# A two-layer decoder trunk: the gate and up products of the feed-forward by Strassen's scheme, with weight sums formed by accumulating DMAs

## The chip, the cores and the metric

The kernel runs on one core of one Trainium2 chip. The metric is the device time of one execution in microseconds, the median of several runs. The engines are TensorE (PE; PEld is its loading of weights), VectorE (DVE), ScalarE (ACT), GpSimd (POOL) and SyncE (SP, which here only issues transfers). All data are float32; products are made of operands split into a high and a low part of the type fp32r, with three matmuls (high x high, high x low, low x high) for each product.

## The reference

Two layers work on x, 512 tokens of 1024 features: each is a mixer, a norm, a feed-forward product and another norm. The change is in the feed-forward:

```python
def swiglu(x, w_gate, w_up, w_down):
    return (jax.nn.silu(x @ w_gate) * (x @ w_up)) @ w_down
...
for layer in range(DEPTH):                      # DEPTH = 2
    ...                                         # mixer: y from x
    x = layer_norm(ALPHA * x + y, ln_mix_g[layer], ln_mix_b[layer])
    x = layer_norm(ALPHA * x + swiglu(x, ffn_w_gate[layer], ffn_w_up[layer], ffn_w_down[layer]),
                   ln_ffn_g[layer], ln_ffn_b[layer])
```

w_gate and w_up are 1024 x 2816, w_down is 2816 x 1024. The 2816 hidden features are 22 tiles of 128 (KF = 22); the 1024 input features are 8 tiles (KD = 8).

## The kernel before, in words

x is kept transposed, features on partitions, as a high part `xh` and a low part `xl`, each 128 x 8 x 512, and in natural layout as `xn`. Weights come as pieces of 128 x 1024 (512 KB) in the order of their use. `fetch` loads the next one on SP's queue into one of five `raw` buffers; `split` has ACT cast it to the high part and DVE subtract that from the raw piece for the low part (lines 94 and 100; on POOL for the first three pieces after a norm, line 98); a pair of high and low lies in one of five `w` buffers.

In `ffn`, a hidden tile needs a gate piece and an up piece. `gemm_a` (line 176) makes the 24 matmuls of a piece, 8 input tiles by three parts, into one PSUM bank of 128 features x 512 tokens. The first two hidden tiles are done in halves of 256 tokens, because the last two blocks of tokens come late from the mixer's norm: the steps `flips` that transpose those blocks stand between their matmuls. The other 20 tiles take 48 matmuls of 512 columns each. `finish` makes the SwiGLU of the two banks (ACT's tanh, line 319, two operations on DVE, lines 320 and 321) and writes the hidden tile: the first eight to the large tile `m8`, the others to `wk` slots of 128 x 512. Then `down` (line 281) takes the hidden tiles as weights, in natural layout, and ends with the residual and `layer_norm`, whose `flip` transposes a finished block on TensorE, casts it from the bank on ACT (line 267) and subtracts on DVE (line 268).

TensorE works in the order in which the program is written. The order of the instructions on the other engines is laid down by a planner at compile time, from costs that it assumes; on the chip each engine then works in that fixed order and stops at an instruction whose operands are not there. Transfers are issued in order on the queue of the engine that starts them. There are eight PSUM banks.

Of the kernel before, what the change touches and what calls it, by code (L numbers as in the profile page):

```python
# [10 lines left out]
F32 = mybir.dt.float32  # L11
# [3 lines left out]
ALU = mybir.AluOpType  # L15
# [14 lines left out]
LOW = -3e38  # L30
VSTAT = (2, 3)  # the blocks whose norm takes its statistics on VectorE, not ScalarE
POOL = 3  # weights split on GpSimd after a norm
WARM = 8  # products of zeros that raise TensorE's clock while the first operands load
RAW, WP, WK, HX = 5, 5, 14, 11
LEVELS = (64, 32, 16, 8, 4, 2, 1)
# [8 lines left out]
def trunk(ctx, tc, a, out):  # L44
# [13 lines left out]
    tmp = ctx.enter_context(tc.tile_pool(name="tmp", bufs=4))  # L58
    sm = ctx.enter_context(tc.tile_pool(name="sm", bufs=4))
    psp = ctx.enter_context(tc.tile_pool(name="psp", bufs=8, space=bass.MemoryType.PSUM))  # L60

    cnt = [0]

    def nm(s):
        cnt[0] += 1
        return f"{s}{cnt[0]}"
# [9 lines left out]

    def small(shape, tag):
        return sm.tile(shape, F32, tag=tag, name=nm(tag))

    def ps():  # L80
        return psp.tile([P, 512], F32, tag="ps", name=nm("ps"))

# [1 line left out]
    state = {"i": 0, "pool": 0}  # L84
# [28 lines left out]
    def weave(*lists):  # L113
        """one order for several lists of steps, each spread evenly"""
        steps = [((i + 0.5) / len(l), n, f) for n, l in enumerate(lists) for i, f in enumerate(l)]
        for _, _, f in sorted(steps, key=lambda x: x[:2]):
            f()

# [1 line left out]
    xh = big.tile([P, KD, S], F32R, name="xh")  # L120
# [3 lines left out]
    def begin(banks):  # L124
        """the first two products, fed piece by piece as x and their weights arrive"""
        raws = [rawp.tile([P, D], F32, tag="raw", name=nm("raw")) for _ in range(2)]
        state["i"] = 2
        ws = [pair(), pair()]

        def load_w(f, half):  # L130
            c = slice(half * 512, half * 512 + 512)
            src = raws[f][:, c]
            nc.sync.dma_start(out=src, in_=a["w"][0, :, f * D + half * 512:f * D + half * 512 + 512])
            split(src, ws[f][0][:, c], ws[f][1][:, c])

# [12 lines left out]
        load_x(1)  # L148
        gemm_a(banks[0], ws[0], ks=(1,))
        load_w(1, 0)  # L150
        gemm_a(banks[1], ws[1], ks=(0, 1))
        for k in (2, 3):
            load_x(k)
            for f in range(2):
                gemm_a(banks[f], ws[f], ks=(k,))
        load_w(0, 1)
        load_w(1, 1)
        for k in range(4, KD):
            load_x(k)
            for f in range(2):  # L160
                gemm_a(banks[f], ws[f], ks=(k,))
        w = weight()
        nc.sync.dma_start(out=pack, in_=a["pack"])
        nc.sync.dma_start(out=wgate, in_=a["wgate"])
        nc.sync.dma_start(out=lm, in_=a["lmask"])
        nc.gpsimd.tensor_copy(out=lmask, in_=lm)
        tsc(out=nsink, in0=sinks, scalar1=-1.0, scalar2=None, op0=ALU.mult)
        return w

# [1 line left out]
    def gemm_a(dst, w, cols=slice(0, S), ks=range(KD)):  # L171
        """dst[128 features, tokens] += w^T x"""
        hi, lo = (t.rearrange("p (k m) -> p k m", k=KD) for t in w)
# [5 lines left out]
    def pieces_a(then, w=None):  # L179
        """two steps of a product whose bank goes to then()"""  # L180
        got = {}
# [10 lines left out]
    def pieces_b(n, then, first=1):  # L192
        """natural layout: a step for each block of tokens (or the first few together),
        x w with 128 tokens and n features"""
        ws = []
# [27 lines left out]

    def layer_norm(b, acc, gb, last):
        """the norm of a block; returns the step that transposes it"""
        g, be = gb
# [32 lines left out]
        def flip():  # L259
            for h in range(2):  # L260
# [6 lines left out]
                nc.scalar.copy(out=xh[dst], in_=tv)  # L267
                tt(out=xl[dst], in0=tv, in1=xh[dst].bitcast(F32), op=ALU.subtract)  # L268
        return flip

    def down(hs, groups, gb, last=False, after=None):
        """natural layout product over the tiles hs, the residual and the norm;
        returns the steps that transpose the last two blocks"""
        nk = len(hs)
# [16 lines left out]
        for gi, size in enumerate(groups):  # L291
            parts = [prep(k) for k in range(k0, k0 + size)]
            k0 += size
            for b in range(NB):
# [11 lines left out]
                if k0 == nk:  # L306
                    flips.append(layer_norm(b, acc[b], gb, last))
        state["pool"] = POOL
        return flips

    def ffn(layer, last, flips):
        gb = load_ln("ffn", layer)
        m8 = big.tile([P, 8, S], F32, tag="m8", name=nm("m8"))
        hs = []

        def finish(f, pg, pu):
            h = m8[:, f, :] if f < 8 else slot()
            t = temp()
# [7 lines left out]
        for f in range(2):  # L326
            for part in range(2):
# [4 lines left out]
                gemm_a(bank, w, cols=slice(0, 256), ks=range(4, KD))  # L332
                first.append((w, bank))
        for f in range(2):
            for w, bank in first[2 * f:2 * f + 2]:
                gemm_a(bank, w, cols=slice(256, 512))
            finish(f, first[2 * f][1], first[2 * f + 1][1])
        with tc.issue_after(norm.ins):
            w = weight()
        for f in range(2, KF):  # L340
            pg, pu = ps(), ps()
            gemm_a(pg, w or weight())
            w = None
            gemm_a(pu, weight())
            finish(f, pg, pu)
        return down(hs, [1] * (KF - 5) + [5], gb, last)

# [1 line left out]
    def mixer0():  # L349
# [113 lines left out]
        weave(att[1:], fill[4:])  # L463
        return down([mix[:, i, :] for i in (4, 5, 6, 7, 0, 1, 2, 3)], [4, 4], gb)

# [1 line left out]
    def rms_scale(ss, n, w):  # L467
# [6 lines left out]
    def mixer1(flips):  # L474
        mix = big.tile([P, 8, S], F32, tag="m8", name=nm("m8"))
        # latent projections, natural layout: [c_q 256 | c_kv 128 | k_r 32 | g_low 16]
        cq = [(slot2(F32R), slot2(F32R)) for _ in range(2)]
# [4 lines left out]
        def latent(b, bank):  # L482
# [10 lines left out]
            kr = mi[:, 384:416]  # L493
            t1, t2 = small([P, 32], "kr1"), small([P, 32], "kr2")
            nc.gpsimd.tensor_tensor(out=t1, in0=kr, in1=kcos[:, b, :], op=ALU.mult)
# [39 lines left out]

        # decay: log-sigmoid, summed within each block of 128
        bb = [slot2(), slot2()]
# [16 lines left out]

        # up-projections; the norms' gains scale the weights' rows
        def scaled(n, parts):
# [47 lines left out]

        # latent attention: a unit is a block of queries and two heads
        def latent_unit(i, hp):
# [76 lines left out]

        # gated linear attention: within blocks of 128, halves against halves at every scale,
        # each with exponents taken from the last token of the first half
        at = [slot2() for _ in range(4)]
        for h in range(4):  # sums of logarithms are never above 0: zeros
            nc.vector.tensor_scalar(out=at[h], in0=bb[h // 2], scalar1=0.0, scalar2=None, op0=ALU.is_gt)
# [47 lines left out]

        dq = small([P, 16], "dq")
        qb, kd = [slot(), slot()], [slot(), slot()]
        dec = [small([P, 4], "dec0"), small([P, 4], "dec1")]

# [94 lines left out]
        for c in range(3):  # L835
# [11 lines left out]
        return down([mix[:, i, :] for i in (4, 5, 6, 7, 0, 1, 2, 3)], [4, 4], gb,  # L847
                    after=[lambda: output_flip(2), lambda: output_flip(3)])

# [14 lines left out]
    sel, bgate, gqn, gkvn = view["sel"], view["bgate"], view["gqn"], view["gkvn"]  # L864
    wgate = const.tile([16, 256], F32, name="wgate")
    nl = len(LEVELS) - 1
# [7 lines left out]

# [1 line left out]
def _chunks(w_in0, w_out0, w_in1, w_out1, wg, wu, wd, uq, ukv):  # L876
# [20 lines left out]
    def ffn(layer):  # L897
        for f in range(KF):
            feat(wg[layer][:, f * P:(f + 1) * P])
            feat(wu[layer][:, f * P:(f + 1) * P])  # L900
        rows(wd[layer])

# [94 lines left out]
```

## Time and profile before

| | |
|---|---|
| median of 3 runs | 1127.43 us (1127.05 to 1130.11) |
| span of the profiled execution | 1126.6 us |
| TensorE busy, granted clock | 1111.4 us (99%), 0.996 |
| DVE, ACT, POOL busy | 549.8, 377.1, 79.2 us |
| moved by DMA | 109.18 MB, 97 GB/s on average |

The span is that of one execution seen by the profiler; the time of a run lies some tenths of a microsecond above it. In the rows of the profile, a group stands as line, engine, operation, output <- input, shapes and count, then busy time and mean duration in ns, then the idle time of the engine just before and what ended it. A timeline row is start, length, engine, line, operation. The chain is the work that ended last, followed back from the end; its rows are start, length, what.

### The profile page before, as it was taken

How to read it: one execution, taken by the hardware profiler on the slowest of the kernel's cores; microseconds unless marked ns; L12 is line 12 of the kernel's file. 1: busy time of each engine (PE TensorE's matmuls, PEld its weight loads, DVE VectorE, ACT ScalarE, POOL GpSimd, SP SyncE). 2: the span in 40 equal slices, each digit the busy share in tenths (PEclk: the TensorE clock that was granted, in tenths of full speed). 3: DMA queues.
4: the chain of work that ended last, by engine and by line, in shares of the span. 5: the costliest groups of instructions: out<-in, count | busy, mean ns of one | idle time of the engine just before them, and what ended most of it. 6: DMA issues, size and time to landing. Idle time of an engine off the chain costs nothing.

```text
span 1126.6 us, 13694 instructions
## 1 busy us (share of the span) xinstructions
PE 1111.4 (99%) x5488; PEld 928.2 (82%) x5488; DVE 549.8 (49%) x910; ACT 377.1 (33%) x660; POOL 79.2 (7%) x108
## 2 busy tenths in 40 slices
PE   9999999999999999999999999999999999999997
PEld 7888888988888888888887888889888888888885
DVE  5755438543333333334857794576433333333337
ACT  4533424322222222223457453443222222222221
POOL 0000013000000000000422420030000000000001
PEclk9999999999999999999999999999999999999999
DMA  9421121422232222222232030224222222222202
GB/s 350 165 75 62 70 75 63 163 94 94 94 108 97 94 94 94 105 100 76 79 141 78 3 113 1 87 74 176 94 94 109 95 95 94 94 100 106 94 1 75
DMA packets 31487, 109.18 MB, mean 97 GB/s; under 512 B 3504, under 2 KB 3648, under 8 KB 31424
## 3 DMA queue, kind: packets, MB, share of 16 engines
q1 hardware_dynamic: 31424, 108.31, 26.6%
q8 instruction: 43, 0.70, 0.3%
q14 instruction: 20, 0.16, 0.0%
HBM read 106.20 MB, written 2.10 MB: 96 GB/s over the span
## 4 chain that ended last, share of the span: by engine, by line
PE 89%; DVE 7%; ACT 1%; issue 1%; DMA 0%; POOL 0%; DVEq 0%; SPq 0%; ACTq 0%; POOLq 0%
PE ps L176 52%; PE ps L281 26%; PE ps L210 5%; PE ps L420 1%; DVE xn L255 1%; PE ps L379 1%; DVE w L100 1%; DVE p L252 1%; DVE p L231 1%; DVE xl L268 1%; PE ps L726 1%; PE ps L408 1%; DVE st L234 1%; DVE hx L735 0%; DMA hx<-in_xT_dram 0%
## 5 line engine op out<-in xcount | busy, mean ns | idle before, releaser
L176 PE MATMUL ps<-xh,w 128*128 128x512 f32 (+1 forms) x1888 | 558.8, 377 | 0.8 <-ACT xh L94 0.8
L176 PEld LDWEIGHTS ps<-xh,w 128*128 128x128 f32 x1888 | 346.4, 188 | 67.7 <-ACT xh L94 1.5
L176 PE MATMUL ps<-xl,w 128*128 128x512 f32 (+1 forms) x944 | 354.1, 375 | 0.7 <-DVE xl L268 0.5
L281 PE MATMUL ps<-w,hx 128*128 128x512 f32 x1440 | 329.4, 390 | 0.0
L281 PEld LDWEIGHTS ps<-w,hx 128*128 128x128 f32 x1440 | 269.7, 188 | 55.6
L94 ACT CAST w<-raw 128x1024 fp32r<-128x1024 f32 (+2 forms) x184 | 189.6, 1039 | 337.0 <-PE ps L281 160.4
L100 DVE TENSOR_TENSOR w<-raw,w 128x1024 fp32r<-128x1024 f32 (+1 forms) x175 | 212.2, 1217 | 63.4 <-ACT w L94 63.3
L176 PEld LDWEIGHTS ps<-xl,w 128*128 128x128 f32 x944 | 177.8, 188 | 32.4 <-DVE xl L268 0.9
L320 DVE SCALAR_TENSOR_TENSOR tmp<-tmp,ps 128x512 f32<-128x512 f32 x44 | 30.2, 688 | 152.2 <-ACT tmp L319 152.2
L319 ACT ACTIVATE tmp<-ps 128x512 f32<-128x512 f32 x44 | 26.3, 598 | 180.4 <-PE ps L176 180.4
L249 POOL TENSOR_TENSOR rs<-ve,neghalf 128x1 f32<-128x1 f32 x16 | 11.5, 718 | 741.8 <-DVE ve L247 711.3
L100 DVE TENSOR_TENSOR hx<-wk,hx 128x512 fp32r<-128x512 f32 x28 | 19.4, 692 | 82.9 <-PE ps L281 82.9
L210 PE MATMUL ps<-w,xh 128*128 128x512 f32 (+1 forms) x192 | 58.1, 383 | 0.0
L321 DVE SCALAR_TENSOR_TENSOR wk<-tmp,ps 128x512 f32<-128x512 f32 x28 | 19.2, 687 | 74.1 <-PE ps L176 74.1
L100 DVE TENSOR_TENSOR hx<-m,hx 128x512 fp32r<-128x512 f32 x32 | 21.7, 687 | 48.0 <-PE ps L281 37.5
L98 POOL TENSOR_TENSOR w<-raw,w 128x512 fp32r<-128x512 f32 (+1 forms) x18 | 28.2, 1594 | 168.5 <-ACT w L94 166.7
L210 PEld LDWEIGHTS ps<-w,xh 128*128 128x128 f32 x192 | 35.5, 188 | 5.3
L210 PE MATMUL ps<-w,xl 128*128 128x512 f32 (+1 forms) x96 | 36.3, 378 | 0.0
L231 DVE SCALAR_TENSOR_TENSOR p<-xn,ps 128x512 f32<-128x512 f32 x32 | 21.8, 680 | 15.6 <-PE ps L281 15.6
L252 DVE SCALAR_TENSOR_TENSOR p<-p,neg,lng 128x512 f32<-128x512 f32 x32 | 25.8, 825 | 5.9 <-ACT ps L245 5.9
L255 DVE SCALAR_TENSOR_TENSOR xn<-p,rs,lnb 128x512 f32<-128x512 f32 x32 | 26.7, 876 | 2.0 <-POOL rs L249 1.4
L321 DVE SCALAR_TENSOR_TENSOR m<-tmp,ps 128x512 f32<-128x512 f32 x16 | 11.0, 688 | 32.1 <-PE ps L176 31.8
(178 smaller groups left out, 678.4 us busy)
## 6 DMA issues: line engine op xcount, KB each, us to landing
raw<-in_w_dram SPq DMA_DIRECT2D x182, 512.0 KB, 3.4
hx<-in_xT_dram SPq DMA_DIRECT2D x8, 256.0 KB, 5.4
xn<-in_xn_dram SPq DMA_DIRECT2D x4, 512.0 KB, 8.4
out_dram<-xn SPq DMA_DIRECT2D x8, 256.0 KB, 2.1
raw<-in_w_dram SPq DMA_DIRECT2D x4, 256.0 KB, 5.4
lng<-in_ln_mix_g_dram SPq DMA_DIRECT2D x2, 512.0 KB, 7.4
lnb<-in_ln_mix_b_dram SPq DMA_DIRECT2D x2, 512.0 KB, 7.5
lng<-in_ln_ffn_g_dram SPq DMA_DIRECT2D x2, 512.0 KB, 3.6
```

Of the source, the lines that this page charges most:

```text
L94: nc.scalar.copy(out=hi, in_=src)
L98: nc.gpsimd.tensor_tensor(out=lo[:, c], in0=src[:, c], in1=hi[:, c].bitcast(F32), op=ALU.subtract)
L100: tt(out=lo, in0=src, in1=hi.bitcast(F32), op=ALU.subtract)
L176: mm(dst[:, cols], lhsT=l[:, k, :], rhs=r[:, k, cols], start=(k == 0 and n == 0), stop=(k == KD - 1 and n == 2))
L210: mm(banks[b][:, :n], lhsT=l[:, k, t], rhs=r[:, c], start=(k == 0 and m == 0), stop=(k == KD - 1 and m == 2))
L231: stt(out=r[h], in0=xn[:, b, h * 512:h * 512 + 512], scalar=ALPHA, in1=acc[h], op0=ALU.mult, op1=ALU.add)
L252: stt(out=r[h], in0=r[h], scalar=neg, in1=g[:, hs], op0=ALU.add, op1=ALU.mult)
L255: state["ln"] = stt(out=xn[:, b, hs], in0=r[h], scalar=rs, in1=be[:, hs], op0=ALU.mult, op1=ALU.add)
L281: mm(acc[b][h], lhsT=l[:, bs], rhs=r[:, h * 512:h * 512 + 512], start=(k == 0 and n == 0), stop=(k == nk - 1 and n == 2))
L319: act(out=t, in_=pg, func=AF.Tanh, scale=0.5)
L320: stt(out=t, in0=t, scalar=1.0, in1=pg, op0=ALU.add, op1=ALU.mult)
L321: stt(out=h, in0=t, scalar=0.5, in1=pu, op0=ALU.mult, op1=ALU.mult)
```

## The change

Hidden tiles 2 to 21 are taken in pairs. For a pair, the gate's and the up's weights (1024 inputs x 256 features each) are stacked as a 2 x 2 block matrix of quarters, by halves of the inputs (0 and 1) and by gate and up; x is cut likewise by halves of the inputs and of the tokens (A11, A21 the tokens below and above 256 for inputs 0 to 511; A12, A22 for inputs 512 to 1023). Instead of eight products of quarters, seven are made, in the form with fewest additions, of sums of quarters on both sides.

- A product is 24 times two: 2 feature tiles x 4 input tiles x 3 parts, matmuls of 256 columns into the halves of a bank.
- Sums on the weights' side: the raw piece stays in its buffer after its split, and an accumulating DMA on POOL's queue adds the next quarter from memory to it; then it is split again. The buffer x takes b11, +b12, +b22, +b21; the buffer y takes b22, +b12; the buffer z takes b21. These are three loads and four accumulating DMAs of 512 KB per pair, in place of four loads. The host lays the pieces out by quarters (`_chunks`; b11 and b21 are the gate's, b12 and b22 the up's). These sums are additions only: the signs lie in x's sums and in the factor -0.5 of the outputs.
- Sums on x's side are formed once per layer on DVE from a transposed x that isn't split: `flip` copies each bank into `xT`, which shares the tile `m8`, and `sums` makes s1 = A22 - A21, s4 = A22 - A21 + A11 - A12, s3 = A11 - A21, each split into high and low in `hx` slots (12 now, 11 before), and s2 = -(A22 - A21 + A11), written over A21 in `xh` and `xl` once the first two tiles are done.
- Sums of the results are made from the banks: two products that are to be added share a bank, after the first one has been copied out on ACT; the others are added on DVE.
- Hidden tiles now go to `wk` slots first (14) and then to `m8`. The matrix `wgate` of mixer 1 is loaded there into a `wk` slot, and not at the start. Four small tiles have fewer buffers. The weights of the products inside `seven` are never split on POOL.

The diff, cut to its core:

```diff
-RAW, WP, WK, HX = 5, 5, 14, 11
+RAW, WP, WK, HX = 5, 5, 14, 12
+DIRECT = 2
...
         nc.sync.dma_start(out=pack, in_=a["pack"])
-        nc.sync.dma_start(out=wgate, in_=a["wgate"])
...
                 nc.scalar.copy(out=xh[dst], in_=tv)
                 tt(out=xl[dst], in0=tv, in1=xh[dst].bitcast(F32), op=ALU.subtract)
+                if keep:
+                    nc.scalar.copy(out=keep()[dst], in_=tv)
...
+    def piece(i, out, add=False):
+        src = a["w"][i // 2, :, (i % 2) * D:(i % 2) * D + D]
+        if add:
+            nc.gpsimd.dma_start(out=out, in_=src, accum_op=ALU.add)
+        else:
+            nc.sync.dma_start(out=out, in_=src)
+
+    def sums():
...
+        for j in range(2):
...
+            q, r = three(temp()), three(temp("p"))
+            tt(out=q, in0=a22, in1=a21, op=ALU.subtract)
+            split(q, out["s1"][0][j], out["s1"][1][j])
+            tt(out=q, in0=q, in1=a11, op=ALU.add)
+            tt(out=r, in0=q, in1=a12, op=ALU.subtract)
+            split(r, out["s4"][0][j], out["s4"][1][j])
+            r = three(temp("p"))
+            tt(out=r, in0=a11, in1=a21, op=ALU.subtract)
+            split(r, out["s3"][0][j], out["s3"][1][j])
+            late.append(q)
+
+        def last_sum():
+            for j in range(2):
+                h, l = out["s2"][0][j], out["s2"][1][j]
+                act(out=h, in_=late[j], func=AF.Copy, scale=-1.0)
+                stt(out=l, in0=late[j], scalar=-1.0, in1=h.bitcast(F32), op0=ALU.mult, op1=ALU.subtract)
+        return out, last_sum
...
+        sx, last_sum = sums()
         for f in range(2):
             for w, bank in first[2 * f:2 * f + 2]:
                 gemm_a(bank, w, cols=slice(256, 512))
             finish(f, first[2 * f][1], first[2 * f + 1][1])
-        with tc.issue_after(norm.ins):
-            w = weight()
-        for f in range(2, KF):
-            pg, pu = ps(), ps()
-            gemm_a(pg, w or weight())
-            w = None
-            gemm_a(pu, weight())
-            finish(f, pg, pu)
+        last_sum()
+        for f in range(DIRECT, KF, 2):
+            seven(f, sx, hs, hidden_tile, norm if f == DIRECT else None)
...
+    def seven(f, sx, hs, hidden_tile, norm):
...
+        def make(name, add=None):
+            if add is not None:
+                piece(add, raw[name], add=True)
+            hi, lo = pair()
+            split(raw[name], hi, lo)
+            return [t.rearrange("p (f k m) -> p f k m", f=2, k=4) for t in (hi, lo)]
...
+        def product(bank, w, x, start=True):
+            hi, lo = w
+            for n in range(2):
+                for k in range(4):
+                    for m, (l, r) in enumerate(((hi, x[0]), (hi, x[1]), (lo, x[0]))):
+                        mm(bank[:, n * 256:n * 256 + 256], lhsT=l[:, n, k, :], rhs=r[k // 2][:, k % 2, :],
+                           start=(start and n == 0 and k == 0 and m == 0), stop=(k == 3 and m == 2),
+                           skip_group_check=True)
...
+        if norm is not None:
+            with tc.issue_after(norm.ins):
+                load("x", b11)
+        else:
+            load("x", b11)
+        product(pa, make("x"), quarter(0, 0))
+        nc.scalar.copy(out=s, in_=pa)
+        product(pb, make("x", b12), sx["s1"])
+        nc.scalar.copy(out=p5, in_=pb)
+        load("z", b21)
+        product(pa, make("z"), quarter(4, 0), start=False)
+        act(out=t0, in_=pa, func=AF.Tanh, scale=0.5)
+        stt(out=t0, in0=t0, scalar=1.0, in1=pa, op0=ALU.add, op1=ALU.mult)
+        load("y", b22)
+        product(pb, make("y"), sx["s4"], start=False)
+        product(pc, make("y", b12), sx["s3"])
+        nc.scalar.copy(out=p7, in_=pc)
+        tt(out=p7, in0=p7, in1=p5, op=ALU.add)
+        product(pd, make("x", b22), sx["s2"])
+        tt(out=s, in0=s, in1=pd, op=ALU.add)
+        tt(out=up0, in0=s, in1=pb, op=ALU.add)
+        tt(out=p7, in0=p7, in1=s, op=ALU.add)
+        product(pc, make("x", b21), quarter(4, 256), start=False)
+        tt(out=s, in0=s, in1=pc, op=ALU.add)
+        act(out=t1, in_=s, func=AF.Tanh, scale=0.5)
+        stt(out=t1, in0=t1, scalar=1.0, in1=s, op0=ALU.add, op1=ALU.mult)
+        for n in range(2):
...
+            stt(out=h[:, 0:256], in0=t0[:, c], scalar=-0.5, in1=up0[:, c], op0=ALU.mult, op1=ALU.mult)
+            stt(out=h[:, 256:512], in0=t1[:, c], scalar=-0.5, in1=p7[:, c], op0=ALU.mult, op1=ALU.mult)
+            hs.append(h)
...
-        return down([mix[:, i, :] for i in (4, 5, 6, 7, 0, 1, 2, 3)], [4, 4], gb)
+        return down([mix[:, i, :] for i in (4, 5, 6, 7, 0, 1, 2, 3)], [4, 4], gb, keep=whole)
```

More of the change, by code (lines that the diff above doesn't have):

```diff
@@ L59, in trunk @@
     sm = ctx.enter_context(tc.tile_pool(name="sm", bufs=4))
+    sm2 = ctx.enter_context(tc.tile_pool(name="sm2", bufs=2))
+    sm1 = ctx.enter_context(tc.tile_pool(name="sm1", bufs=1))
     psp = ctx.enter_context(tc.tile_pool(name="psp", bufs=8, space=bass.MemoryType.PSUM))
@@ L75, in temp, with small @@
         return tmp.tile([P, 512], dt, tag=tag, name=nm(tag))
-    def small(shape, tag):
-        return sm.tile(shape, F32, tag=tag, name=nm(tag))
+    def small(shape, tag, pool=None):
+        return (pool or sm).tile(shape, F32, tag=tag, name=nm(tag))
     def ps():
@@ L222, in load_ln, with layer_norm @@
         return g, b
-    def layer_norm(b, acc, gb, last):
+    def layer_norm(b, acc, gb, last, keep=None):
         g, be = gb
@@ L268, in flip, with down @@
                 tt(out=xl[dst], in0=tv, in1=xh[dst].bitcast(F32), op=ALU.subtract)
+                if keep:
+                    nc.scalar.copy(out=keep()[dst], in_=tv)
         return flip
-    def down(hs, groups, gb, last=False, after=None):
+    def down(hs, groups, gb, last=False, after=None, keep=None):
         nk = len(hs)
@@ L306, in down, with whole @@
                 if k0 == nk:
-                    flips.append(layer_norm(b, acc[b], gb, last))
+                    flips.append(layer_norm(b, acc[b], gb, last, keep))
         state["pool"] = POOL
         return flips
+    def whole():
+        if "xT" not in state:
+            state["xT"] = big.tile([P, KD, S], F32, tag="m8", name=nm("m8"))
+        return state["xT"]
+    def piece(i, out, add=False):
[4 more added lines that the diff above has]
+            nc.sync.dma_start(out=out, in_=src)
@@ new lines, in sums, with three @@
+    def sums():
+        xT = state.pop("xT")
+        out = {n: ([slot2(F32R), slot2(F32R)], [slot2(F32R), slot2(F32R)]) for n in ("s1", "s4", "s3")}
+        out = {n: [[t.rearrange("p (k t) -> p k t", k=2) for t in half] for half in hl] for n, hl in out.items()}
+        out["s2"] = [[t[:, 2 * j:2 * j + 2, 256:] for j in range(2)] for t in (xh, xl)]
+        def three(t):
+            return t.rearrange("p (k t) -> p k t", k=2)
+        late = []
+        for j in range(2):
+            lo_k, hi_k = slice(2 * j, 2 * j + 2), slice(4 + 2 * j, 6 + 2 * j)
+            a11, a21 = xT[:, lo_k, :256], xT[:, lo_k, 256:]
+            a12, a22 = xT[:, hi_k, :256], xT[:, hi_k, 256:]
+            q, r = three(temp()), three(temp("p"))
[14 more added lines that the diff above has]
+        return out, last_sum
@@ L311, in ffn, with hidden_tile @@
     def ffn(layer, last, flips):
         gb = load_ln("ffn", layer)
-        m8 = big.tile([P, 8, S], F32, tag="m8", name=nm("m8"))
         hs = []
+        m8 = {}
+        def hidden_tile(f):
+            if f < WK:
+                return slot()
+            if not m8:
+                m8["t"] = big.tile([P, 8, S], F32, tag="m8", name=nm("m8"))
+            return m8["t"][:, f - WK, :]
         def finish(f, pg, pu):
-            h = m8[:, f, :] if f < 8 else slot()
+            h = hidden_tile(f)
@@ new lines, in ffn, with load, quarter @@
+        return down(hs, [1] * (KF - 5) + [5], gb, last)
+    def seven(f, sx, hs, hidden_tile, norm):
+        i = state["i"]
+        state["i"] += 4
+        b11, b12, b22, b21 = range(i, i + 4)
+        raw = {}
+        def load(name, first):
+            raw[name] = rawp.tile([P, D], F32, tag="raw", name=nm("raw"))
+            piece(first, raw[name])
+        def make(name, add=None):
[4 more added lines that the diff above has]
+            return [t.rearrange("p (f k m) -> p f k m", f=2, k=4) for t in (hi, lo)]
+        def quarter(k0, t0):
+            return [[t[:, k0 + 2 * j:k0 + 2 * j + 2, t0:t0 + 256] for j in range(2)] for t in (xh, xl)]
+        def product(bank, w, x, start=True):
[6 more added lines that the diff above has]
+                           skip_group_check=True)
+        pa, pb, pc, pd = ps(), ps(), ps(), ps()
+        s, p5, p7, up0 = temp(), temp("p"), temp("p"), temp("p")
+        t0, t1 = temp(), temp()
+        if norm is not None:
[25 more added lines that the diff above has]
+        for n in range(2):
+            h = hidden_tile(f + n)
+            c = slice(n * 256, n * 256 + 256)
+            stt(out=h[:, 0:256], in0=t0[:, c], scalar=-0.5, in1=up0[:, c], op0=ALU.mult, op1=ALU.mult)
+            stt(out=h[:, 256:512], in0=t1[:, c], scalar=-0.5, in1=p7[:, c], op0=ALU.mult, op1=ALU.mult)
+            hs.append(h)
@@ L493, in latent @@
             kr = mi[:, 384:416]
-            t1, t2 = small([P, 32], "kr1"), small([P, 32], "kr2")
+            t1, t2 = small([P, 32], "kr1", sm2), small([P, 32], "kr2", sm2)
             nc.gpsimd.tensor_tensor(out=t1, in0=kr, in1=kcos[:, b, :], op=ALU.mult)
@@ L534, in mixer1 @@
         nc.vector.tensor_copy(out=glT[0:16, :], in_=prg[32:48, :])
+        wgate = slot()[0:16, :256]
+        nc.sync.dma_start(out=wgate, in_=a["wgate"])
         bb = [slot2(), slot2()]
@@ L735, in level @@
                     nc.vector.copy_predicated(dst, mask[:, None, :, :].broadcast_to([P, NB, 64 // L, L]), src)
-        dq = small([P, 16], "dq")
+        dq = small([P, 16], "dq", sm1)
         qb, kd = [slot(), slot()], [slot(), slot()]
-        dec = [small([P, 4], "dec0"), small([P, 4], "dec1")]
+        dec = [small([P, 4], "dec0", sm1), small([P, 4], "dec1", sm1)]
         def diagonal():
@@ L847, in mixer1 @@
         return down([mix[:, i, :] for i in (4, 5, 6, 7, 0, 1, 2, 3)], [4, 4], gb,
-                    after=[lambda: output_flip(2), lambda: output_flip(3)])
+                    after=[lambda: output_flip(2), lambda: output_flip(3)], keep=whole)
     neghalf = const.tile([P, 8], F32, name="neghalf")
@@ L864, in trunk @@
     sel, bgate, gqn, gkvn = view["sel"], view["bgate"], view["gqn"], view["gkvn"]
-    wgate = const.tile([16, 256], F32, name="wgate")
     nl = len(LEVELS) - 1
@@ L897, in ffn @@
     def ffn(layer):
-        for f in range(KF):
+        for f in range(DIRECT):
             feat(wg[layer][:, f * P:(f + 1) * P])
             feat(wu[layer][:, f * P:(f + 1) * P])
+        for f in range(DIRECT, KF, 2):
+            for w, half in ((wg, 0), (wu, 0), (wu, 1), (wg, 1)):
+                quarter = w[layer][half * 512:half * 512 + 512, f * P:(f + 2) * P]
+                pieces.append(quarter.reshape(4, P, 2, P).transpose(1, 2, 0, 3).reshape(P, D))
         rows(wd[layer])
```

## The prediction

> **What bounds the kernel now.** I read the page first, its busy shares, slices and queues; then the chain that ended last; then, inside the stage that the change rewrites, the timeline by engine, the windows and the groups by shape.
>
> ```profile
> span 1126.6 us, 13694 instructions
> ...
> PE 1111.4 (99%) x5488; PEld 928.2 (82%) x5488; DVE 549.8 (49%) x910; ACT 377.1 (33%) x660; POOL 79.2 (7%) x108
> ...
> PEclk9999999999999999999999999999999999999999
> ...
> q1 hardware_dynamic: 31424, 108.31, 26.6%
> q8 instruction: 43, 0.70, 0.3%
> q14 instruction: 20, 0.16, 0.0%
> ```
>
> TensorE is busy all the time at its full clock; no other engine is near its limit. The queues hold plain hardware transfers only: no accumulating transfer and no transfer of POOL's software queue occurs, so that price will have to be bounded.
>
> ```profile
> 201.76 229.29 PE ps L176 x1055
> 431.05 110.16 PE ps L281 x486
> 769.73 229.28 PE ps L176 x1055
> ```
>
> In the chain (start, length, what) the gate and up products of each layer are one unbroken run of matmuls of 229 us; the down products follow at once. Shortening this stage means giving TensorE fewer or cheaper matmuls. Their pitches, from the timeline of TensorE (both rows are the middle one of a group of three) and of ACT (the tanh of one feature tile and of the next):
>
> ```profile
> 202.22 0.28 PE L176 MATMUL ps<-xl,w 128*128 128x256 f32 x1
> ...
> 213.02 0.28 PE L176 MATMUL ps<-xl,w 128*128 128x256 f32 x1
> ...
> 213.50 0.40 PE L176 MATMUL ps<-xl,w 128*128 128x512 f32 x1
> ```
>
> ```profile
> 229.81 0.60 ACT L319 ACTIVATE tmp<-ps 128x512 f32<-128x512 f32 x1 [3.83 <-PE ps L176]
> ...
> 240.69 0.60 ACT L319 ACTIVATE tmp<-ps 128x512 f32<-128x512 f32 x1 [3.83 <-PE ps L176]
> ```
>
> Of 256 columns: 10.80 us for 30 groups of three, so 120.0 ns each. Of 512 columns: 10.88 us for the 48 matmuls of a tile, so 226.7 ns each. Half of 226.7 is 113.3, so halving the columns wastes 6.7 ns per matmul, far less than an eighth.
>
> **TensorE's term.** A pair of feature tiles takes 2 x 2 x 24 = 96 matmuls of 512 columns, 2 x 10.88 = 21.76 us. Seven products take 7 x (2 tiles x 4 k x 3 parts) = 168 matmuls of 256 columns, each with its own weight load like the rows at 202 to 213, so 168 x 0.120 = 20.16 us, 2.88 per product. Ten pairs in each of two layers: 20 x 1.60 = 32.0 us less, all on the chain. Break-even is a pitch of 21.76 / 168 = 129.5 ns. The Trainium skill, "TensorE: Matmul & The Clock Gate", section "Back-to-back issue gap", gives columns / 2.4 + 2.5 ns for isolated matmuls: 215.8 and 109.2 ns, by which the gain would be an estimated 47 us. The trace is 11 ns above both, so the measured 32 stands.
>
> **Splits, sums and outputs beside TensorE.** Durations by shape:
>
> ```profile
> L100 DVE TENSOR_TENSOR w<-raw,w 128x1024 fp32r<-128x1024 f32 x170 | 207.5, 1225 | 59.1 <-ACT w L94 59.1
> ...
> L94 ACT CAST w<-raw 128x1024 fp32r<-128x1024 f32 x176 | 183.7, 1051 | 327.7 <-PE ps L281 154.2 <-PE ps L176 118.7 <-issue 53.1
> ...
> L320 DVE SCALAR_TENSOR_TENSOR tmp<-tmp,ps 128x512 f32<-128x512 f32 x44 | 30.2, 688 | 152.2 <-ACT tmp L319 152.2
> ...
> L319 ACT ACTIVATE tmp<-ps 128x512 f32<-128x512 f32 x44 | 26.3, 598 | 180.4 <-PE ps L176 180.4
> ...
> L706 DVE TENSOR_TENSOR tmp<-tmp,hx 128x256 f32<-128x256 f32 x14 | 6.1, 443 | 0.0
> ...
> L410 ACT COPY hx<-ps 128x512 f32<-128x512 f32 x8 | 4.8, 597 | 1.7 <-PE ps L408 1.7
> ```
>
> A pair has 7 splits instead of 4. DVE: 7 x 1.23, five sums and two products of 512 columns at 0.69, four products of 256 at 0.44: 15.2 of 20.16 us. ACT: 7 x 1.05, three bank copies and two tanh at 0.60: 10.4 us. Both fit behind TensorE, so I cost them at nothing; without that cover DVE would set 15.2 us a pair and still not lose. The three bank copies are new waits of TensorE, since a bank is copied out before the next product adds to it. One product lies between in each case, 2.88 us against 0.60.
>
> **Transfers.** Before, a pair needs four loads; now three on SP's queue and four accumulating ones on POOL's, 7 x 512 KB.
>
> ```profile
> 250.00:400.00 150.00, 150.00 (x663) 124.26 (x662) 52.78 (x56) 36.79 (x43) 0.00 (x0) 1.00 0.27 98
> ```
>
> ```profile
> raw<-in_w_dram SPq DMA_DIRECT2D x182, 512.0 KB, 3.4
> hx<-in_xT_dram SPq DMA_DIRECT2D x8, 256.0 KB, 5.4
> xn<-in_xn_dram SPq DMA_DIRECT2D x4, 512.0 KB, 8.4
> ...
> wgate<-in_wgate_dram SPq DMA_DIRECT2D x1, 16.0 KB, 6.3
> ```
>
> The window's last two columns are DMA share and GB/s: 98 GB/s at 0.27 means 363 GB/s at full share, so 524 KB occupy the 16 engines for 1.45 us. Let an accumulating transfer occupy them for a. It can't be under 1.45, since it moves the same bytes in; it also reads its destination, which no row here prices. From above I bound it by three passes, 4.4: read, read back and write, each at a plain load's time. I take two passes, 2.9, nearest to the load row, whose bytes it moves once and reads once more: 3 x 1.45 + 4 x 2.9 = 16.0 us of 20.16, hidden. The Trainium skill, "Collectives: The Full Stack", section "Why ReduceScatter is half of AllGather", puts the cost of a reducing transfer in its second read, not in the add, half the rate; by that too a is an estimated 2.9. No run here shows it.
>
> Its time from issue to landing, L, lies between 3.4 (the plain weight load) and 8.4 (same size, queued behind others). I take 5.5: the nearest row plus another 1.45 of engine time and some waiting. In the x buffer the order is split, add, split, add, split, add, split; in y split, add, split. Split buffers are five deep, so product n's split may start when product n-5 has ended. An add between neighbouring products then has 5 x 2.88 = 14.4 us for two splits of 1.05 + 1.23 and L: it is hidden while L is under 9.8. POOL has no other work in this window (0.00 above); an add waiting on POOL's queue holds up only later adds. SP's three loads are fewer than the four of before.
>
> That margin asks that ACT and DVE, which run in order, do not stand at a split that waits for an add while others are ready. The planner does move work ahead of its program order:
>
> ```profile
> 208.79 0.61 ACT L94 CAST hx<-m 128x512 fp32r<-128x512 f32 x1
> ```
>
> This split belongs to the down products, written after the whole gate and up loop, and runs 222 us ahead of them. So I expect the splits of z and y in the gaps. Behind a stuck split on ACT would queue the bank copies, and behind those TensorE.
>
> **Around the stage.** In each mixer's end every flip gains two copies of a bank into the whole transposed x. The last flip before:
>
> ```profile
> 199.57 1.08 ACT L267 CAST xh<-ps 128x512 fp32r<-128x512 f32 x2 [5.59 <-PE ps L263]
> ```
>
> ```profile
> 201.02 1.28 DVE L268 TENSOR_TENSOR xl<-ps,xh 128x512 fp32r<-128x512 f32 x2
> ```
>
> ```profile
> 201.17 20.91 SPq L90 DMA_DIRECT2D raw<-in_w_dram  x6
> 201.76 0.19 PEld L176 LDWEIGHTS ps<-xl,w 128*128 128x128 f32 x1 [0.45 <-DVE xl L268]
> 201.76 0.39 PE L176 MATMUL ps<-xl,w 128*128 128x256 f32 x1 [0.25 <-DVE xl L268]
> ```
>
> A copy between the two casts delays the second xl, for which TensorE waits, by 0.60 us; 0 if it runs after both, 1.2 if both come first. I take 0.6, twice: 1.2 us. Then DVE forms the sums: 14 operations of 0.69, 9.7 us, beside two weight splits and two tiles' outputs (2.5 + 2.8): 15 us from 201.8, to 216.8. TensorE has direct columns until 213.5 and product 0 until 216.4; the sum that product 1 needs is DVE's first. The first chain of adds starts cold: load issued 201.2, landed 204.6, split 206.9, added 212.4, split 214.7, second add split 222.5, third 230.3, needed at 230.8. It fits by 0.5, on a busy DVE. I charge 1.5 per layer (0 to 4): 3.0 us. The last sum overwrites a quarter of xh that no later product reads, and waits for the direct products; needed at 227.9. At the stage's end the down products' first split tiles wait for sum tiles; the first four are free five products, 14 us, earlier: nothing, else 1.3 us. The gate matrix's load moves from the start into mixer 1: it waits for a work tile on SP's queue, ahead of the next weights, with many matmuls to cover it; uncovered at most 6.3. Fewer small buffers: nothing.
>
> **Sum.** 1126.6 - 32.0 + 1.2 + 3.0 = 1098.8 us of span. The median of the runs, 1127.43, is 0.8 above the profiled span, so 1099.6 us. About 0.3% (3.4 us) is what a measurement of this kernel can tell from no change.
>
> **Rivals.**
> 1. *Accumulating transfers fill the DMA engines (slower).* The stage then takes 3 x 1.45 + 4a per pair. From a = 3.95 they set the pace, and from 4.3 the gain is gone. At 4.7 it is 23.2 us: 20 x 3.0 = 61 more than forecast, 1160. For it: no row prices the read-back. Against it: 1.45 must triple.
> 2. *The in-order queue (slower).* If ACT and DVE take the seven splits in program order, three adds stand exposed: about 4.4 + 3.3 + 3.3 us of splits plus 3 L. Already at L = 3.6 this reaches 21.76; at 5.5 it is 27.5 us, 20 x 7.3 = 147 more, about 1247. For it: a static order made for another L than the chip's. Against it: the row at 208.79.
> 3. *Partly starved.* L near 9.8 or bank copies late by one product's slack leave holes of about 0.5 to 1.2 us a pair: 1110 to 1124, still faster.
> 4. *The pitch does not hold* for banks written in halves: at 125 ns a pair takes 21.0 and the time is 1116. The stage at 202 to 213 writes halves of banks too, at 120, so I give it little, inside rival 3.
>
> **How the numbers follow.** TensorE sets the pace: 0.55, own range 1093 (no edge charges) to 1108. Rival 3 with 4: 0.09. Within 0.3%: 0.06, a balance of gain and starving. Rival 1: 0.16, rival 2: 0.14. Hence faster 0.64, same 0.06, slower 0.30. The range must reach into the slower cases: up to 1155 it takes about half of rival 1 and a third of rival 2 in a mild form, leaving out some 0.18.
>
> **What would show it.** Right: 168 matmuls per pair at 120 ns without gaps, a stage of about 215 us (229.3 - 16 + 1.5), DVE near 75% and DMA near 0.8 there. Wrong: waits of TensorE for the split's cast or subtraction that lead back to an accumulating transfer; adds above 9 us to landing; a DMA share at 0.95 (rival 1), or a low share with ACT standing at a cast (rival 2).

## The result, and the profile after

The changed kernel takes 1367.69 us (median of 4 runs, 1364.65 to 1369.44) against 1128.77 before on the same chip: 1.2106 times as long, 95% interval 1.208 to 1.2132. The forecast was 1099.6 us. The page of the changed kernel, its busy shares, slices, queues and the chain by engine:

```profile
span 1367.7 us, 17278 instructions
...
PE 1192.0 (87%) x6928; PEld 1058.9 (77%) x6928; DVE 701.1 (51%) x1142; ACT 488.5 (36%) x812; POOL 147.0 (11%) x188
...
PEclk9999999888888888999999999998888888889999
...
q1 hardware_dynamic: 28544, 97.82, 21.4%
q0 software_dynamic: 11520, 41.95, 18.7%
...
PE 44%; DMA 25%; issue 20%; DVE 8%; ACT 3%; POOL 0%; POOLq 0%; DVEq 0%; SPq 0%; ACTq 0%
```

TensorE is no longer always busy, its clock is below full in both gate and up stages, and a quarter of the chain is now DMA. The stage that took 229 us takes 347 (203 to 550):

```profile
203.00:550.00 347.00, 267.78 (x1787) 255.81 (x1786) 157.72 (x203) 111.12 (x141) 33.77 (x39) 0.86 0.51 109
```

The added 118 us per layer are nearly the whole loss. No engine is near its limit there, and the DMA share, the last but one column, is 0.51: rival 1, full DMA engines, is out. The transfers' issues (size, median us to landing), from the groups of DMA issues:

```profile
raw<-in_w_dram SPq DMA_DIRECT2D x162, 512.0 KB, 3.9
raw<-in_w_dram POOLq DMA_DIRECT2D x80, 512.0 KB, 6.4
```

Where the time goes is to be seen on ACT's timeline over one pair, 33.3 us from the copy at 317.61 to that at 350.92, and on POOL's queue with the adds that these casts wait for:

```profile
317.61 0.58 ACT L445 COPY tmp<-ps 128x512 f32<-128x512 f32 x1
318.08 2.00 ACT L97 CAST w<-raw 128x1024 fp32r<-128x1024 f32 x2
321.94 0.59 ACT L447 COPY p<-ps 128x512 f32<-128x512 f32 x1 [1.85 <-PE ps L431]
324.82 0.60 ACT L450 ACTIVATE tmp<-ps 128x512 f32<-128x512 f32 x1 [2.29 <-PE ps L431]
329.35 1.99 ACT L97 CAST w<-raw 128x1024 fp32r<-128x1024 f32 x2 [3.94 <-DMA raw<-in_w_dram]
336.81 0.59 ACT L455 COPY p<-ps 128x512 f32<-128x512 f32 x1 [5.46 <-PE ps L431]
339.73 1.99 ACT L97 CAST w<-raw 128x1024 fp32r<-128x1024 f32 x2 [2.33 <-DMA raw<-in_w_dram]
345.94 0.63 ACT L463 ACTIVATE tmp<-tmp 128x512 f32<-128x512 f32 x1 [4.21 <-DVE tmp L462]
349.96 1.04 ACT L97 CAST w<-raw 128x1024 fp32r<-128x1024 f32 x1 [3.40 <-DMA raw<-in_w_dram]
350.92 0.58 ACT L445 COPY tmp<-ps 128x512 f32<-128x512 f32 x1
```

```profile
321.82 0.86 POOL L324 DMA_DIRECT2D raw<-in_w_dram  x1 [1.70 <-DVE w L103]
333.09 0.86 POOL L324 DMA_DIRECT2D raw<-in_w_dram  x1 [10.40 <-DVE w L103]
344.06 0.86 POOL L324 DMA_DIRECT2D raw<-in_w_dram  x1 [10.11 <-DVE w L103]
```

The compiled order of ACT gives these casts their names (a list of instructions, not of times; `raw_2618` is x, `raw_2677` z, `raw_2708` y):

```
L463 ACTIVATE tmp_2390<-tmp_2385     tanh of the pair before
L97 CAST w_2649<-raw_2618            x'
L445 COPY tmp_2612<-ps_2608
L97 CAST w_2679<-raw_2677            z
L97 CAST w_2710<-raw_2708            y
L447 COPY p_2613<-ps_2609
L450 ACTIVATE tmp_2616<-ps_2608
L97 CAST w_2738<-raw_2708            y'
L97 CAST w_2768<-raw_2618            x''
L455 COPY p_2614<-ps_2610
L97 CAST w_2799<-raw_2618            x'''
L97 CAST w_2847<-raw_2845            x of the next pair
```

The seven casts stand in exactly the order of the program; so do those of the other pairs. Three times per pair ACT stands at a cast whose buffer is still being added to: y' at 329.35 (its add issued at 321.82), x''' at 339.73 (333.09), x' at 349.96 (344.06). From issue to cast these are 7.53, 6.64 and 5.90 us, 20.1 together; the other 13.2 of the 33.3 us are splits and hand-overs between them. Over the whole kernel ACT waits 61 times for a transfer at such a cast, where 20 pairs with three waits each make 60 (us in total, times, longest):

```profile
ACT w L97 <- DMA raw<-in_w_dram: 174.0, 61, 5.0
```

TensorE then waits for the cast:

```profile
330.45 0.50 PE L431 MATMUL ps<-hx,w 128*128 128x256 f32 x2 [2.79 <-ACT w L97]
```

### The profile page after: what moved, and what is told of

The parts are those of the page before. It is cut to its first block, busy times and chain, and to the rows that moved or that the text cites. A ratio compares the mean times of both kernels' runs of the same rounds, so it can differ in the third digit from the quotient of the medians.

```text
span 1367.7 us, 17278 instructions
## 1 busy us (share of the span) xinstructions
PE 1192.0 (87%) x6928; PEld 1058.9 (77%) x6928; DVE 701.1 (51%) x1142; ACT 488.5 (36%) x812; POOL 147.0 (11%) x188
## 3 DMA queue, kind: packets, MB, share of 16 engines
q1 hardware_dynamic: 28544, 97.82, 21.4%
q0 software_dynamic: 11520, 41.95, 18.7%
## 4 chain that ended last, share of the span: by engine, by line
PE 44%; DMA 25%; issue 20%; DVE 8%; ACT 3%; POOL 0%; POOLq 0%; DVEq 0%; SPq 0%; ACTq 0%
DMA raw<-in_w_dram 24%; PE ps L285 21%; PE ps L178 10%; PE ps L212 5%; DVE w L103 3%; ACT w L97 2%; PE ps L544 1%; PE ps L503 1%; DVE tmp L458 1%; PE ps L852 1%; DVE xn L257 1%; PE ps L431 1%; PE ps L699 1%; DVE p L254 1%; DVE p L233 1%
## 5 line engine op out<-in xcount | busy, mean ns | idle before, releaser
L103 DVE TENSOR_TENSOR w<-raw,w 128x1024 fp32r<-128x1024 f32 (+1 forms) x235 | 281.9, 1218 | 209.7 <-ACT w L97 209.6
L431 PE MATMUL ps<-xh,w 128*128 128x256 f32 x1280 | 279.7, 313 | 62.9 <-ACT w L97 48.1
L431 PE MATMUL ps<-hx,w 128*128 128x256 f32 x1440 | 238.5, 329 | 95.0 <-ACT w L97 66.2
L97 ACT CAST w<-raw 128x1024 fp32r<-128x1024 f32 (+2 forms) x244 | 245.5, 1038 | 204.0 <-DMA raw<-in_w_dram 174.0
L431 PEld LDWEIGHTS ps<-hx,w 128*128 128x128 f32 x1440 | 220.2, 233 | 110.5 <-ACT w L97 73.7
L431 PE MATMUL ps<-xl,w 128*128 128x256 f32 x640 | 197.1, 308 | 0.0
L178 PE MATMUL ps<-xh,w 128*128 128x512 f32 (+1 forms) x608 | 165.8, 353 | 1.1 <-ACT xh L97 1.1
L431 PEld LDWEIGHTS ps<-xl,w 128*128 128x128 f32 x640 | 140.1, 219 | 0.0
L324 POOL DMA_DIRECT2D raw<-in_w_dram x80 | 69.5, 869 | 613.1 <-DVE w L103 589.4
L178 PE MATMUL ps<-xl,w 128*128 128x512 f32 (+1 forms) x304 | 105.6, 347 | 0.0
L178 PEld LDWEIGHTS ps<-xl,w 128*128 128x128 f32 x304 | 58.1, 191 | 6.7 <-DVE xl L103 0.4
L101 POOL TENSOR_TENSOR w<-raw,w 128x512 fp32r<-128x512 f32 (+1 forms) x18 | 27.5, 1557 | 169.1 <-ACT w L97 169.1
```

The costliest lines, as they stand in the source:

```text
L97: nc.scalar.copy(out=hi, in_=src)
L101: nc.gpsimd.tensor_tensor(out=lo[:, c], in0=src[:, c], in1=hi[:, c].bitcast(F32), op=ALU.subtract)
L103: tt(out=lo, in0=src, in1=hi.bitcast(F32), op=ALU.subtract)
L178: mm(dst[:, cols], lhsT=l[:, k, :], rhs=r[:, k, cols], start=(k == 0 and n == 0), stop=(k == KD - 1 and n == 2))
L324: nc.gpsimd.dma_start(out=out, in_=src, accum_op=ALU.add)
L431: mm(bank[:, n * 256:n * 256 + 256], lhsT=l[:, n, k, :], rhs=r[k // 2][:, k % 2, :], start=(start and n == 0 and k == 0 and m == 0), stop= ...
```

## The experiments

The theory after the result: each pair waits for three adds in full, because ACT works through its casts in the order of the program (rival 2). Against it stood the rate of the transfers, and TensorE's clock.

**Loads without a chain.**

```diff
-                piece(add, raw[name], add=True)
+                load(name, add)
```

> The four accumulating DMAs of a pair become plain loads on SP's queue, each into a fresh raw buffer: the weight sums are left out, everything else (seven splits, 168 matmuls, sums on x, outputs) stays, and no transfer waits for a split of its own pair. Order theory (splits stand in program order on ACT and each of three adds per pair is waited for in full): no exposed add is left, so a pair falls to TensorE's 20.2 us and the kernel to about 1100 us (1095 to 1110). Rate theory (seven transfers of 512 KB per pair, with or without read-back, are too much for the DMA engines): seven plain loads of 1.57 us are 11 us per pair, also hidden, so this run does not tell the two apart, but a time above 1150 would speak for a third cause on the engines or in TensorE's clock.

1101.57 us (1101.21 to 1101.94), ratio to before 0.9762 (0.9731 to 0.9794). The sums are left out here, and the casts of the splits keep their order among themselves. The same casts, the same matmuls and as many transfers cost no time of TensorE's in this stage once no transfer has to wait for a split of its own pair: TensorE, second column, is never idle, and the DMA share is higher than in the slow kernel.

```profile
250.00:400.00 150.00, 150.00 (x1252) 150.00 (x1252) 108.47 (x137) 73.77 (x90) 0.00 (x0) 1.00 0.56 182
```

**The same chain with plain transfers.**

```diff
-            nc.gpsimd.dma_start(out=out, in_=src, accum_op=ALU.add)
+            nc.gpsimd.dma_start(out=out, in_=src)      # e2;  e3: nc.sync.dma_start
```

> The four adds become plain copies on the same POOL queue into the same buffers, so each still waits for the split before it and the next split still waits for it; the sums are left out, and so is the read-back. Order theory: a pair takes 13.2 us of splits and hand-overs plus three landing times; with a plain landing on that queue of 4.5 to 5.5 us instead of 6.6 it is 27 to 30 us, 1230 to 1300 us in all. Rate theory: without read-back seven transfers take 11 us of the DMA engines per pair, TensorE sets the pace, about 1100 us.

> As the run before, but the four plain copies go on SP's queue, whose 512 KB loads landed after 3.9 us. Order theory: 13.2 + 3 x 3.9 = 24.9 us per pair, 20 x 8.4 us less than after, about 1200 us; more if loads of the next pair stand behind a copy that waits on SP's queue. Rate theory: about 1100 us.

1262.78 us (1260.17 to 1265.40) and 1259.11 us (1254.24 to 1263.97). The rate theory asked for 1100 in both. On POOL's queue the plain copy landed after 4.6 us:

```profile
raw<-in_w_dram POOLq DMA_DIRECT2D x80, 512.0 KB, 4.6
```

A pair took 28.9 us there (six copies of line 445 between 273.68 and 418.34), against 34.0 in the changed kernel (five such copies between 282.71 and 418.83): 5.1 us less for three landings shorter by 1.8 each, which would give 5.4. The copies on SP's queue came out at 29.0 us per pair and about 60 us above what I expected for them. In the pair from 299.78 to 329.19 us they took 5.59, 5.60 and 4.81 us from issue to cast, where 3.9 each was expected. Only the second of these casts waited for its transfer; before the others ACT stood at work that waited for TensorE. So this run gives no third point for the landing.

**Products interleaved.** All adds stay; each pair's products and splits are placed at seven of ten positions, and a new pair starts every seven:

```diff
-        for f in range(DIRECT, KF, 2):
-            seven(f, sx, hs, hidden_tile, norm if f == DIRECT else None)
+        todo = []
+        for f in range(DIRECT, KF, 2):
+            i = (f - DIRECT) // 2
+            todo += [(7 * i + p, g) for p, g in seven(f, ...)]
+        for _, g in sorted(todo, key=lambda x: x[0]):
+            g()
...
+        return [(0, x0), (1, y0), (3, x1), (4, z0), (5, y1), (6, x2), (9, x3)]
```

Here `x0` splits x and starts its add at once, `x1` splits the sum, and so on; `y0` has a bank of its own.

> All sums and all 80 accumulating DMAs stay; only the order is new: the products of neighbouring pairs interleave, so that three products stand between one split of a buffer and the next (x at positions 0, 3, 6, 9, y at 1 and 5, z at 4, a new pair every 7). One product gets a bank of its own, and one bank copy goes. Order theory: 3 x 2.88 = 8.6 us nearly cover split, landing and split (2.5 + 6.6), so a pair takes 20.2 to 21.3 us; with one exposed add of about 7 us at each layer's end 1110 to 1140 us. Rate theory: the same transfers, the same time as after, about 1368 us.

1107.54 us in two runs; again, with four runs:

> The interleaved kernel again, with enough rounds for an interval: 1103 to 1110 us, 2% faster than before. The adds take 3.2 us of the DMA engines each, so with the loads they fill 0.86 of them in the stage; if that is too near to full, single runs scatter by several us.

1107.56 us (1104.59 to 1109.11), ratio 0.9811 (0.9791 to 0.9831): faster than before, and below the 1110 to 1140 us of the first expectation; whether by 2% these runs leave open. The 80 adds are all there and still land 5.9 us after their issue (median) in the first of these profiles. ACT's waits for them between 300 and 345 us are 1.5 to 1.8 us each, and TensorE is busy without a gap from 250 to 400 us. On POOL's queue a pair now goes by in 19.8 us (the first row to the last), close to TensorE's 20.16:

```profile
304.54 0.86 POOL L324 DMA_DIRECT2D raw<-in_w_dram  x1 [7.25 <-DVE w L103]
306.95 0.86 POOL L324 DMA_DIRECT2D raw<-in_w_dram  x1 [1.55 <-DVE w L103]
309.87 0.86 POOL L324 DMA_DIRECT2D raw<-in_w_dram  x1 [2.06 <-DVE w L103]
316.07 0.86 POOL L324 DMA_DIRECT2D raw<-in_w_dram  x1 [5.33 <-DVE w L103]
324.37 0.86 POOL L324 DMA_DIRECT2D raw<-in_w_dram  x1 [7.44 <-DVE w L103]
```

**Only the order of the splits.** TensorE's order, its banks and the transfers as in the changed kernel:

```diff
+            order = (cut["x1"], prod[0], cut["y1"], prod[1], cut["x2"], prod[2], nxt.get("x0"), prod[3],
+                     cut["x3"], prod[4], nxt.get("z"), prod[5], nxt.get("y0"), prod[6])
```

> TensorE's order, banks and all transfers as in the changed kernel; only the order in which the splits are written is new: per pair x', y', x'', x of the next pair, x''', z and y of the next pair, and each add is written right behind the split it waits for. Order theory: what costs is the fixed order of the casts, not the products' order. Two or three splits now stand between a split and the one that needs its add; y to y' and x' to x'' have one between, x'' to x''' one. With 2.5 us for a split and 6.4 for a landing, the cycle x' (after y), y' , x'', x''' comes to about 22 us per pair against 33.3: 1115 to 1165 us. If TensorE's order or the shared banks were the cause: about 1368 us.

1185.79 us (1183.84 to 1187.74), ratio 1.0507 (1.048 to 1.0535). So 182 of the 239 us that the change lost come back by moving the splits, and the adds behind them, alone; the order is the cause. It is 20 us slower than the range I gave. One pair of this run on ACT shows why: three casts still wait (4.68, 6.66 and 2.81 us), as only one split stands between y and y', x' and x'', x'' and x'''.

```profile
306.55 2.00 ACT L97 CAST w<-raw 128x1024 fp32r<-128x1024 f32 x2 [4.68 <-DMA raw<-in_w_dram]
...
318.33 1.05 ACT L97 CAST w<-raw 128x1024 fp32r<-128x1024 f32 x1 [6.66 <-DMA raw<-in_w_dram]
...
323.19 1.05 ACT L97 CAST w<-raw 128x1024 fp32r<-128x1024 f32 x1 [2.81 <-DMA raw<-in_w_dram]
```

**A third of the matmuls left out.**

```diff
-                    for m, (l, r) in enumerate(((hi, x[0]), (hi, x[1]), (lo, x[0]))):
+                    for m, (l, r) in enumerate(((hi, x[0]), (lo, x[0]))):
```

> The changed kernel with two of three matmuls in each of the seven products (the part of high weights by low x is left out): 112 matmuls per pair, 13.4 us of TensorE at full clock in place of 20.2. Order theory: TensorE is not on the path in this stage, a pair stays at 32 to 34 us, 1330 to 1370 us in all. Clock theory (the granted clock falls to half in the gaps, and the slowed products, some 5 us each in place of 2.9, are what makes the stage long): a third of the slowed work goes, 20 x 6 us or more, 1250 us or less.

1334.32 us (1331.68 to 1336.95). A pair took 32.1 us (four pairs between the copies at 276.95 and 405.15), two less than with all matmuls, where 6.7 us of TensorE's work at full clock were left out. The granted clock even fell to 0.74 in this window (column after the five engines; 0.86 in the changed kernel), and the kernel was faster all the same:

```profile
250.00:400.00 150.00, 97.86 (x521) 91.97 (x519) 63.32 (x81) 44.63 (x55) 15.53 (x18) 0.74 0.53 116
```

So TensorE and its clock are only a part of the path in the slow stage: a third of the matmuls was worth 2 of the 34 us.

**Two moves at the stage's start.** Both on the interleaved kernel:

```diff
                 if keep:
-                    nc.scalar.copy(out=keep()[dst], in_=tv)
+                    late.append((dst, tv))
+            for dst, tv in late:
+                nc.scalar.copy(out=keep()[dst], in_=tv)
```

and the sums s3 for both halves behind those for s1 and s4.

> The interleaved kernel with two small moves: in a flip both casts of xh come before the two copies for the whole transposed x, and the sums for s3 are formed after those for s1 and s4, which its product order needs first. If the copies between the casts cost what the prediction charged (0.6 us per layer, up to 1.2) and the wait for s4 about 1 us, it is 2 to 4 us faster than the interleaved kernel, 1099 to 1105 us; if the norm's chain on DVE hides the copies, no difference.

1102.95 us (1101.57 to 1103.21), ratio 0.9769 (0.9754 to 0.9784), 4.6 us below the interleaved kernel of the same chip. TensorE still waited at the start of that kernel's stage, and in its chain a transfer of 5.72 us stood ahead of the first pair; these rows are gone with the two moves. Which of the two did it was not tried. One of TensorE's waits in the interleaved kernel (185 to 432 us) and the transfer in its chain, and then the chain with the moves:

```profile
PE ps L435 <- ACT hx L97: 1.1, 1, 1.1
```

```profile
213.39 5.72 DMA raw<-in_w_dram
```

```profile
202.63 12.96 PE ps L178 x108
215.58 201.60 PE ps L440 x1680
417.18 110.19 PE ps L288 x486
```

**The gate matrix earlier.** In the chain of the last kernel the moved 16 KB load stood with 3.6 us:

```profile
574.31 3.60 DMA wk<-in_wgate_dram
```

```diff
     def mixer1(flips):
+        wgate = slot()[0:16, :256]
+        nc.sync.dma_start(out=wgate, in_=a["wgate"])
...
-        wgate = slot()[0:16, :256]
-        nc.sync.dma_start(out=wgate, in_=a["wgate"])
```

> The interleaved kernel with the late copies, and the 16 KB load of the gate matrix written at the start of mixer 1 instead of behind its first products. In the interleaved kernel that load, behind a weight load on SP's queue, stood on the chain for 3.6 us, and mixer 1 (from the end of the down run to the start of the next one) took 182.5 us against 179.7 before. If the moved load is what those 2.8 us are, 1099 to 1101 us. If mixer 1 lost them elsewhere, no difference from 1103 us.

> The interleaved kernel with the late copies again, on the same chip as the run beside it: 1101 to 1104 us.

1099.90 us (1099.29 to 1101.04) and, for the same kernel without the early load, 1100.96 (1098.58 to 1103.31). These runs can tell no difference. That the first lies in its range therefore says nothing for the moved load, since the second came out just below its own. The load left the chain, but mixer 1, from the end of the down run to the run of 72 down matmuls, took 179.7 us with the early load and 180.0 without in this profile (182.5 in the profile of the same kernel in the run before). So in these two profiles what lies beside the load is nearly as long.

The lowest median is that of the interleaved version with both moves and the early load: ratio to before 0.9748 (0.9730 to 0.9767), with the same products and the same adds that took 1367.7 us in the first order.

## Why the prediction was wrong, step by step

- *TensorE's term, right.* The pitch of 120.0 ns held wherever TensorE was not starved: the row of 1680 matmuls above is 201.60 us, 168 x 0.120 x 10 to the digit. Rival 4 is out. With the chain taken out, the first experiment came within 2 us of the forecast of 1099.6.
- *The step that failed* is "The planner does move work ahead of its program order ... So I expect the splits of z and y in the gaps." The row shown for it was a cast of the down products that had nothing to wait for. From that I took that a cast which must wait would be passed over. The compiled order did not do it for a single one of the seven casts, and ACT stands where the order says: three times a pair, 20.1 of 33.3 us from issue to cast. What length the planner assumed for an add no run shows. That this order is what costs is shown by the run in which another order alone gave back 182 us.
- *Rival 2 had the mechanism, not the size.* It was given 0.14 and 27.5 us per pair. Measured are 33.3 in the pair shown: from issue to cast it took 6.7 on average instead of 5.5 (3 x 1.2 = 3.6 us), and splits with their hand-overs 13.2 instead of 11.0 (2.2). The break-even of this rival, L = 3.6 us, lies below the median landings on POOL's queue, 6.4 with the add and 4.6 without. With 13.2 it is an estimated 2.9 us ((21.76 - 13.2) / 3), below the 3.4 to 4.3 us of the loads on SP's queue too. In program order this chain could not win with any of these transfers. The sentence on the break-even stood in the text and should have carried more weight than one row of another cast.
- *The margin of 9.8 us for an add, not tested.* It took splits to run ahead as far as the five split buffers allow, and no run shows that. In the interleaved order three products, 3 x 2.88 = 8.6 us, stand between dependent splits instead, and there adds that landed after 5.9 us left TensorE no gap.
- *The price of an add, nearly right.* 18.7% of 1367.7 us over 80 adds is 3.2 us of the 16 engines, where 2.9 was taken. 21.4% over 97.82 MB is 1.57 us for a plain load, so an add costs 2.0 times as much. The Trainium skill, "Collectives: The Full Stack", section "Why ReduceScatter is half of AllGather", puts a reducing transfer at half the rate for its second read; the trace agrees on the factor, and no run here shows the second read itself. Interleaved, the DMA share in the stage is 0.80 (the row below), as the sum said.
- *Engines beside TensorE, right.* DVE was forecast at 15.2 of 20.16 us (75%); in the interleaved kernel with the moves it is 163.13 of 213 us (77%):

```profile
203.00:416.00 213.00, 213.00 (x1777) 213.00 (x1777) 163.13 (x210) 106.41 (x131) 33.77 (x39) 1.00 0.80 179
```

- *The edges, about right without the chain.* A layer should have come out 16.0 us shorter less 2.1 for the edges. Before, the down runs of the two layers start at 431.05 and 999.01. In the first experiment, without the chain, they start at 417.14 and 972.85: 13.9 and 12.3 us less in the two layers, so edges of 2.1 and 3.7. In the interleaved kernel they start at 419.66 and 976.55, edges of 4.6 and 4.9. In the version with the moves and the early load they are 1.4 and 1.0, but that version has another order and reworked edges: that its 1099.90 us lies next to the forecast is in part luck. The rows without the chain, and those with the moves and the early load:

```profile
417.14 110.19 PE ps L285 x486
...
972.85 119.72 PE ps L285 x528
```

```profile
416.41 110.19 PE ps L288 x486
...
969.39 119.72 PE ps L288 x528
```

## What to carry to other kernels

Where an in-place chain (split, add by DMA, split) feeds an engine that works in order, write the steps so that as many independent ones stand between two links as the landing takes; five split buffers gave no overlap here as long as the order was the program's. Price such a chain in the order of the program first, and believe in a better order only after having read it in the compiled list of instructions. One load per buffer in place of the chain (the sums left out, the rest as it is) tells in one run what the chain costs.

## What had not been expected of the hardware

After a gap of 3.73 us TensorE's clock was lower for a while: in the changed kernel the matmuls of 256 columns from 309.88 to 312.44 came 213 ns apart instead of 120 (four groups of three in 2.56 us), at a granted clock of 0.50. From 314.17 on they came 120 ns apart again, at 1.00.

```profile
309.88 0.41 PE L431 MATMUL ps<-xl,w 128*128 128x256 f32 x1
...
312.44 0.41 PE L431 MATMUL ps<-xl,w 128*128 128x256 f32 x1
```

An accumulating transfer on POOL's queue lands 2.5 us later than a load on SP's (6.4 against 3.9, medians). About 1.8 of this goes with the accumulation: without it the same transfer on the same queue landed after 4.6.
